# Layer-norm sums over partitions issued for four feature tiles together, one on each quarter of the TensorE array

## Chip, cores and metric

One core of one Trainium2 chip runs the whole program. The metric is the device time of one execution in microseconds (us): the median over several runs. All times below are in us unless marked ns.

## What is computed

The network has two post-norm layers over 256 latent and 256 context tokens with 1024 features. Each layer mixes tokens (a gated linear recurrence, an attention and a Mamba-2 scan, then one output projection) and then applies a SwiGLU feed-forward network (FFN). After each of the two sub-layers the residual stream goes through a layer norm over the 1024 features:

```python
def layer_norm(x, g, b):
    mu = jnp.mean(xf, axis=-1, keepdims=True)
    var = jnp.mean(jnp.square(xf - mu), axis=-1, keepdims=True)
    return ((xf - mu) * lax.rsqrt(var + LN_EPS) * g + b).astype(x.dtype)
...
# x <- LayerNorm(alpha * x + gate * sublayer(x * (1 + scale) + shift))
```

So there are four layer norms in the program. Only the latent tokens are needed behind the attention of the second layer.

## The kernel before, in words

Activations lie feature-major: a feature tile has 128 features on the partitions and the tokens along the free dimension, and 8 such tiles make the 1024 features. In layer 0 a tile has 512 columns (context and latent), in layer 1, behind the mixer, 256 (latent alone). Matrix products are made exact by splitting both operands into two float32r parts (`hh`/`hl`, `yh`/`yl`, `oh`/`ol` for activations, `wh`/`wl` for weights), with three products for each pair. Weight blocks of 128 x 1024 stream in by DMA from the SP queue (line 115) and are split by ACT (line 125, `wh`) and DVE (line 126, `wl`) some blocks ahead. All matmuls are issued by the helper in line 204, all transposes by that in line 208, so that rows are told apart by their tiles.

A layer norm reduces over partitions, which DVE can't. `ln_add` (line 1176) is called once for each feature tile, as soon as the tile of the residual sum has been made from PSUM by DVE (`resid`, line 1145, two scalar_tensor_tensor, one for each half of the tokens). The projection before it makes two tiles at a time, so tiles 0 and 1 come together, then 2 and 3, and so on. Nothing happens for the first three calls. At the fourth, `colmean` (line 880, with `quarters`, line 869) forms the mean of the first four tiles: four float32 matmuls with a 128 x 32 matrix of ones, each to another 32 partitions of one PSUM tile (`csum`), that is, on another quarter of the array's columns, then one matmul that adds the quarters. That mean (`pivot`) is taken off the four tiles and off what is added to the later ones. Then, tile by tile, ACT squares the tile (`sq`), and two float32 matmuls with the same 128 x 32 matrix of ones (`ones32`, printed `ones`) add over partitions: the tile into `lsum`, its square into `lsq`. Tile d goes to the quarter d % 4 of both PSUM tiles:

```python
            q = 32 * (d % 4)
            for ps, t in zip(ln["s"], (x, sq)):
                self.mm(ps[q:q + 32, 0:n], self.ones32, t, d < 4, d >= 4)
```

So a layer norm has 16 such sums, and the program 64. The first four tiles are summed in the fourth call, tiles 4 to 7 in one call each, with products of the projection between them. `raw_split` (line 405) then makes split operands of the tile (`raw`) for products that don't wait for the statistics.

`ln_stats` (line 1199) copies `lsum` (ACT) and `lsq` (DVE) to SBUF, adds the quarters with small matmuls into `lst`, and works out mean and inverse deviation with short DVE instructions (`s`). `ln_end` spreads them over partitions (`spread`). Meanwhile PE runs the products of `raw` (`g<-raw`), whose statistics are put in later. `post_norm` (line 1258) then normalizes tile by tile on DVE, applies gains on ACT and splits into `hh` and `hl` for the products of the next stage. After the first layer's second norm the first stage is the Mamba step sizes (`ssd_dt`, tiles `dx`, `dy`, `dz`), which end in two kinds of transposes on PE (`dtT`). After the last norm, `finish` (line 1369) makes the output token-major: products of the tiles with a diagonal of gains (`g<-dg`, `fin<-dg`), less the mean (`g<-gr,lsum`), scaled and stored.

The code is written as one stream with each engine's part in program order, but the order within each engine's queue is set by the tile framework's scheduler when the program is built: it moves instructions of an engine past each other by its own estimate of when they are ready. At run time each engine takes its queue strictly in that order, and an instruction whose inputs aren't there holds up all behind it.

Of the kernel before, what the change touches and what calls it, by code (L numbers as in the profile page):

```python
# [9 lines left out]
AF = mybir.ActivationFunctionType  # L10
# [5 lines left out]
ND = 8  # L16
# [4 lines left out]
T = SEQ + CTX  # L21
ALPHA = (2 * DEPTH) ** 0.25
FFN = 2816
# [10 lines left out]
# columns of the per-channel parameters of a layer  # L34
# [19 lines left out]
def stagger(a, b, n):  # L54
    """a, and from its step n on b beside it"""
    for _ in range(n):
        next(a, None)
        yield
    live = [a, b]
    while live:  # L60
        for g in list(live):
            if next(g, g) is g:
                live.remove(g)
            else:
                yield
# [6 lines left out]
class Weave:  # L72
    """Two strands of work: the steps of the side strand are spread over those of the main one and stay a
    little behind it, so that the main strand's next products never queue behind the end of a side chain."""
# [4 lines left out]
    def __call__(self, main, side, nm, ns, lead=0, lag=0):  # L79
        """nm and ns: the steps of each, lag: the part of the side strand, in steps of main, left for the next call"""  # L80
        side, n, j = chain(self.side, side), self.n + ns, 0
        for i, _ in enumerate(main):
            while j < n * (i + 1 - lead) / (nm - lead + lag):
                next(side, None)
                j += 1
        self.side, self.n = side, n - j
        if not lag:
            run(side)
            self.n = 0


class Weights:
    """Streams weight blocks [128, k, c] through SBUF: each block is loaded once
    and split into two float32r parts whose sum is the float32 value."""
# [49 lines left out]
class Net:  # L144
# [21 lines left out]
    def x(self, name="x"):  # L166
        """like a, for tiles that would otherwise queue behind the other strand's"""
        return self.wp.tile([P, 512], F32, tag="x", name=name, bufs=self.n_x)
# [45 lines left out]
    def rsqrt(self, x, n):  # L214
        """x <- x ** -1/2 on a few columns: a first guess from the exponent and three Newton steps"""
        y, t = self.s(n), self.s(n)
        self.ts(t.bitcast(I32), x.bitcast(I32), 1, ALU.arith_shift_right)
        self.ts(y.bitcast(I32), t.bitcast(I32), -1, ALU.mult, 0x5F3759DF, ALU.add)
        for i in range(3):
            self.stt(t, y, -0.5, y, ALU.mult, ALU.mult)  # L220
            self.tt(t, t, x, ALU.mult)
            self.stt(x if i == 2 else y, t, 1.5, y, ALU.add, ALU.mult)


# [37 lines left out]
    def lower_bounds(self):  # L262
        """the second layer's: the softmax over two layers as a sigmoid"""
        h = self.s(32)
        self.nc.gpsimd.dma_start(out=h, in_=self.io["lb"])
        self.tt(h[:, 0:16], h[:, 16:32], h[:, 0:16], ALU.subtract)
        self.act(self.lb, h[:, 0:16], AF.Sigmoid)
        self.act(self.lbm, h[:, 0:16], AF.Sigmoid, scale=-1.0)

# [1 line left out]
    def mod_spec(self, l, j, c):  # L271
        """512 columns from 512 j, rows [256 c, 256 c + 256)"""
# [27 lines left out]
    def tick(self):  # L300
        """a piece of the modulations that are needed later"""
# [10 lines left out]
    def load_x(self, d0, d1):  # L312
        """feature-major tokens, [context | latent]"""
# [8 lines left out]
    def modulate_first(self, d0, d1):  # L322
        """h = x (1 + sc) + sh"""
# [23 lines left out]
    def mm3(self, out, xh, xl, yh, yl, first, last):  # L347
        """out += (xh + xl)^T (yh + yl)"""
# [4 lines left out]
    def plan_w(self, key, w, cols, kt=ND):  # L353
        """a unit: 256 columns of a weight matrix, in blocks of four row tiles"""
# [5 lines left out]
    def unit_f(self, key, rng, x=None, kt=ND):  # L360
        """feature-major: two tiles of 128 columns by the tokens rng[m]"""
# [11 lines left out]
    def unit_raw(self, key, ln):  # L373
        """two tiles of 128 columns before the layer norm's statistics are there: products with the rows times
        the gains, and with the gains and biases as two more tokens"""
# [20 lines left out]
    def raw_end(self, ln, e, j):  # L396
        """the statistics put in: a tile but for the bias, and the bias"""
# [7 lines left out]
    def raw_split(self, ln):  # L405
        """the next rows times the gains as split operands, with the gains and biases behind them"""
# [17 lines left out]
    def unit_t(self, key, js):  # L424
        """token-major: pairs js of token tiles by 256 columns"""
# [23 lines left out]
    def hgrn_in(self, l, p, wc, st):  # L449
        """projections of a pair of heads and everything that reads them from PSUM"""  # L450
# [38 lines left out]
    def hgrn_head(self, l, st, m, wc, oh, ol):  # L489
        """One head: attention over all pairs of tokens by levels of halving. At level h a block of 2h tokens  # L490
        is halved; the forward direction reads keys of the first half from queries of the second, the
        backward direction the other way. K = [forward | backward] keys times the decay to the end
        (start) of their half, Q = [backward | forward] queries times the decay over their half."""
# [10 lines left out]
        def total(h):  # L504
            """products of the decays over blocks of h, [forward | backward] of T / h each"""
# [5 lines left out]
        def grow(h):  # L511
            """to halves of 2h"""
# [106 lines left out]
    def ssd_dt(self, l):  # L619
        """step sizes, their logarithms and the decays' running sums, (stream, direction, head) on partitions"""  # L620
# [30 lines left out]
        ln = r  # L651
# [49 lines left out]
    def conv(self, l, r, n, t0):  # L701
        """depthwise conv over time, feature-major"""
# [37 lines left out]
    def silus(self, tiles):  # L740
        """together, after the exponentials before them: one switch of the activation table"""
# [15 lines left out]
    def ssd_scan(self, l, g, st, dts, wc, ys):  # L757
        """both directions' scans of a group: within each stream by its decay matrix, from the context by its end states"""
# [85 lines left out]
    def ssd_out(self, l, g, ys, zs, wc, om):  # L844
        """gate and grouped RMS norm"""
# [23 lines left out]
    def quarters(self, tiles, n):  # L869
        """sum over partitions of every fourth tile, on 32 partitions each"""  # L870
# [9 lines left out]
    def colmean(self, tiles, n):  # L880
        """mean over partitions and tiles, on every partition"""
# [4 lines left out]
    def colrstd(self, tiles, n, scale, eps):  # L886
        """(scale * sum over partitions and tiles + eps) ** -1/2, on every partition"""
# [15 lines left out]
    def rms_tok(self, ps, scale):  # L903
        """(mean square + eps) ** -1/2 * scale of each 128 columns, [token, 4]"""
# [8 lines left out]
    def rotate(self, l, key, src, dst, lat):  # L913
        """gain, and on latent tokens rotary, of [token, (2 tiles, 2 heads, 128)]"""
# [13 lines left out]
    def attn_tables(self, l):  # L928
        """rotary tables with the gains in them"""
# [117 lines left out]
    def partial(self, key, o, dst, first, q0):  # L1047
        """dst += rows block of a projection; o is a function where it isn't there yet"""
# [23 lines left out]
    def gate_first(self, l, acc, q0):  # L1072
        """the gated Mamba branch, to DRAM"""
# [13 lines left out]
    def gates(self, l, br, q0, cs=range(4), f=AF.Sigmoid):  # L1087
        """the gates of a branch that isn't there yet, to DRAM"""
# [11 lines left out]
    def early(self, l, g=None):  # L1100
        """the gates (branch, columns) whose products stand beside the Mamba scan of group g, and all of them"""
# [4 lines left out]
    def gates_on(self, br, q0, cs):  # L1106
        """the sigmoids of gates that were stored before them"""
# [12 lines left out]
    def branch(self, l, br, key, o, q0, out=None):  # L1120
        """a gated branch added to those before it: to DRAM, or into split parts"""
# [23 lines left out]
    def resid(self, l, i, src, d, r, x, q0):  # L1145
        """r = gate * src + x"""
# [20 lines left out]
    PIVOT = 4  # L1167

    def ln_begin(self, q0, x, gains=None):
        """gains: of the layer norm and of what reads it"""  # L1170
        ln = {"q0": q0, "x": x, "r": [], "s": None, "raw": [], "ga": None}
# [4 lines left out]
    def ln_add(self, ln, r):  # L1176
        """The next tile of the rows to normalize. The mean of the first few is taken off all tiles as they
        come: what is left has a mean of the order of its deviation at most, and its sums give the variance."""
# [11 lines left out]
        for d in (range(np) if len(rs) == np else (len(rs) - 1,)):  # L1190
            x = rs[d][:, q0:T]
            sq = self.a(name="sq")[:, 0:n]
            self.act(sq, x, AF.Square)
            q = 32 * (d % 4)
            for ps, t in zip(ln["s"], (x, sq)):
                self.mm(ps[q:q + 32, 0:n], self.ones32, t, d < 4, d >= 4)
        self.raw_split(ln)

    def ln_stats(self, ln):
        """less the mean and the inverse deviation, [token, tile], and the sums they come from"""  # L1200
# [17 lines left out]
    def ln_end(self, ln):  # L1218
        """factor and summand of the normalization, token by token, on every partition"""
# [6 lines left out]
    def spread(self, x, nt):  # L1226
        """columns x [token, nt] to rows on every partition"""
# [11 lines left out]
    def gains(self, ln, l, ig, ib, nxt):  # L1239
        """the layer norm's own, times alpha, and those that lead to the input of what reads it"""  # L1240
# [18 lines left out]
    def post_norm(self, ln, raws):  # L1259
        """the units raws, and the split operand LN * (1 + sc) + sh of what reads it"""  # L1260
# [17 lines left out]
    def new_x(self, ln, q0):  # L1278
        """the residual stream alpha * LN"""
# [80 lines left out]
    def finish_tables(self, l):  # L1360
        """the last layer norm's gains on a diagonal, and its gains and biases as rows"""
# [7 lines left out]
    def finish(self, ln, out):  # L1369
        """the last layer norm, token-major: products with the diagonal of gains, less the mean times the gains"""  # L1370
# [165 lines left out]
def pack(inputs):  # L1536
    """the arrays of the launch: weights as they are, per-channel vectors and tokens with channels first"""
# [35 lines left out]
```

## Time and profile before

| | us |
|---|---|
| median of 3 runs | 2702.61 |
| fastest and slowest run | 2701.3, 2703.74 |
| the profiled execution, span from first to last instruction | 2706.7 |
| PE busy in it | 2619.4 |
| DVE busy | 1782.5 |
| ACT busy | 1232.1 |
| POOL busy | 192.4 |

The profile records one execution. No device time of it is given beside its span, which is 4.1 above the median of the runs. PE is the engine of matmuls, PEld its weight loads, which overlap. Matmuls are pipelined and their ends are modelled: distances between starts are the safe numbers. A float32 matmul of the kind above leaves two records, each with a weight load of its own. A name such as `lsum<-r,ones` says what is written and from what; xN is the number of records that a row merges.

### The profile page before, as it was taken

To read this page: it belongs to the slowest core of one execution; us is meant where nothing else is said; L and a number is where in the kernel's file an instruction comes from. 1 tells how busy PE (TensorE), PEld (TensorE's weight loads), DVE (VectorE), ACT (ScalarE), POOL (GpSimd) and SP (SyncE) were. 2 spreads that over 40 slices of the span, in tenths; PEclk is the share of its full clock that TensorE was granted. 3 is DMA by queue.
4 is the path that set the end of the run, shared out by engine and by line. 5 is a ranking of instruction groups with operands and counts; after the bars stand their busy time and mean duration, and the time that the engine had idled before them with its cause. 6 is when DMAs were issued, how large, how long until landed. Compare 5 with 4: busy or idle time off the path is not lost.

```text
span 2706.7 us, 46300 instructions
## 1 busy us (share of the span) xinstructions
PE 2619.4 (97%) x18660; PEld 2148.0 (79%) x18660; DVE 1782.5 (66%) x3708; ACT 1232.1 (46%) x2030; POOL 192.4 (7%) x320
## 2 busy tenths in 40 slices
PE   7999999999999999999999999899999999999999
PEld 5767767788888897777888877677878898878998
DVE  5887776756555675456433367887867778867555
ACT  3555554532333324535432236566554344465543
POOL 0111010000000001100000000111110011111000
PEclk9999999999999999999999999899999999999999
DMA  6566555543444445352333323555763353445553
GB/s 238 152 179 176 150 164 149 155 123 114 122 135 130 128 125 172 105 175 63 101 94 101 94 78 90 140 164 154 212 183 108 97 144 109 144 131 181 169 182 102
DMA packets 298951, 374.41 MB, mean 138 GB/s; under 512 B 16432, under 2 KB 251984, under 8 KB 298736
## 3 DMA queue, kind: packets, MB, share of 16 engines
q1 hardware_dynamic: 271568, 284.21, 34.9%
q0 software_dynamic: 25728, 84.61, 11.0%
q8 instruction: 147, 2.41, 0.4%
q10 hardware_dynamic: 1440, 2.62, 0.3%
q14 instruction: 68, 0.56, 0.1%
HBM read 355.27 MB, written 16.12 MB: 137 GB/s over the span
## 4 chain that ended last, share of the span: by engine, by line
PE 69%; DVE 6%; DMA 3%; ACT 3%; issue 1%; POOL 0%; DVEq 0%; ACTq 0%; SPq 0%
PE g L204 56%; PE y L204 1%; PE PV L204 1%; PE S L204 1%; DVE wl L126 1%; DMA wraw<-in_w_in 1%; DMA ce<-sd 1%; PE o L204 1%; PE small L204 1%; PE cross L204 1%; PE mod L204 1%; PE PT L208 1%; PE lsq L204 1%; DVE s L196 1%; ACT wh L125 1%
## 5 line engine op out<-in xcount | busy, mean ns | idle before, releaser
L126 DVE TENSOR_TENSOR wl<-wraw,wh 128x1024 fp32r<-128x1024 f32 (+1 forms) x450 | 544.5, 1212 | 430.2 <-ACT wh L125 419.3
L125 ACT ACTIVATE wh<-wraw 128x1024 fp32r<-128x1024 f32 (+1 forms) x450 | 470.9, 1048 | 712.0 <-PE g L204 513.1
L204 PE MATMUL g<-hh,wh 128*128 128x512 f32 (+2 forms) x2032 | 733.5, 363 | 5.4 <-ACT wh L125 2.1
L204 PE MATMUL g<-hh,wl 128*128 128x512 f32 (+2 forms) x2032 | 726.2, 358 | 4.4 <-DVE wl L126 4.4
L204 PE MATMUL g<-hl,wh 128*128 128x512 f32 (+2 forms) x2032 | 725.9, 358 | 0.0
L204 PEld LDWEIGHTS g<-hh,wh 128*128 128x128 f32 (+1 forms) x2032 | 387.9, 191 | 77.4 <-issue 16.0
L204 PEld LDWEIGHTS g<-hh,wl 128*128 128x128 f32 (+1 forms) x2032 | 388.4, 191 | 66.4 <-issue 9.1
L204 PEld LDWEIGHTS g<-hl,wh 128*128 128x128 f32 (+1 forms) x2032 | 388.6, 191 | 61.8 <-issue 12.1
L204 PE MATMUL g<-oh,wh 128*128 128x512 f32 (+1 forms) x864 | 301.3, 350 | 2.6 <-DVE gl L193 1.5
L204 PE MATMUL g<-ol,wh 128*128 128x512 f32 (+1 forms) x864 | 295.6, 343 | 0.2 <-DVE ol L196 0.2
L204 PE MATMUL g<-oh,wl 128*128 128x512 f32 (+1 forms) x864 | 293.1, 340 | 0.5 <-DVE wl L126 0.5
L204 PE MATMUL g<-wh,hh 128*128 128x256 f32 x768 | 221.4, 288 | 0.0
L204 PE MATMUL g<-wh,hl 128*128 128x256 f32 x768 | 220.0, 286 | 0.0
L204 PE MATMUL g<-wl,hh 128*128 128x256 f32 x768 | 218.7, 285 | 0.0
L204 PEld LDWEIGHTS g<-oh,wh 128*128 128x128 f32 x864 | 163.9, 190 | 30.0 <-issue 8.1
L204 PEld LDWEIGHTS g<-ol,wh 128*128 128x128 f32 x864 | 164.3, 190 | 23.4 <-issue 7.1
L204 PEld LDWEIGHTS g<-oh,wl 128*128 128x128 f32 x864 | 163.9, 190 | 21.0 <-issue 3.6
L204 PEld LDWEIGHTS g<-wh,hh 128*128 128x128 f32 x768 | 147.6, 192 | 3.1 <-issue 2.6
L204 PEld LDWEIGHTS g<-wh,hl 128*128 128x128 f32 x768 | 147.7, 192 | 2.2 <-issue 1.9
L204 PEld LDWEIGHTS g<-wl,hh 128*128 128x128 f32 x768 | 147.6, 192 | 0.5 <-issue 0.4
L196 DVE SCALAR_TENSOR_TENSOR u<-craw,vec,u 128x508 f32<-128x508 f32 (+3 forms) x192 | 131.0, 723 | 10.0 <-ACT u L190 8.9
L196 DVE SCALAR_TENSOR_TENSOR D<-ab,tk,neg 128x128 f32<-128x128 f32 x384 | 110.3, 347 | 21.5 <-DMA ab<-sd 21.5
(303 smaller groups left out, 3600.3 us busy)
## 6 DMA issues: line engine op xcount, KB each, us to landing
wraw<-in_w_in SPq DMA_DIRECT2D x216, 512.0 KB, 4.1
wraw<-in_w_mod SPq DMA_DIRECT2D x96, 512.0 KB, 4.1
wraw<-in_w_ffn_in SPq DMA_DIRECT2D x88, 512.0 KB, 3.6
ab<-sd POOLq DMA_DIRECT2D x64, 512.0 KB, 6.9
wraw<-in_w_ffn_out SPq DMA_DIRECT2D x40, 512.0 KB, 3.4
ce<-sd POOLq DMA_DIRECT2D x64, 256.0 KB, 7.6
wraw<-in_w_br_mb SPq DMA_DIRECT2D x32, 512.0 KB, 3.4
wraw<-in_w_in SPq DMA_DIRECT2D x34, 256.0 KB, 3.5
```

Of the source, the lines that this page charges most:

```text
L125: self.nc.scalar.activation(hi[:, 0:n], t[:, 0:n], AF.Copy)
L126: self.nc.vector.tensor_tensor(out=lo[:, 0:n], in0=t[:, 0:n], in1=hi[:, 0:n], op=ALU.subtract)
L196: return self.nc.vector.scalar_tensor_tensor(out=out, in0=a, scalar=s, in1=b, op0=op0, op1=op1)
L204: return self.nc.tensor.matmul(out, l, r, start=start, stop=stop)
L208: return self.nc.tensor.transpose(out, in_, self.ident[0:k, 0:k])
```

## The change

`ln_add` collects the squares, and issues no sums until a fourth tile is there (after the fourth call and after the eighth). Then it issues the four sums of the tiles, quarter after quarter, and the four sums of the squares after them. What is summed, into which PSUM tiles and on which quarters, is the same. Squares, pivot and `raw_split` are issued as before.

```diff
-        ln = {"q0": q0, "x": x, "r": [], "s": None, "raw": [], "ga": None}
+        ln = {"q0": q0, "x": x, "r": [], "s": None, "sq": [], "raw": [], "ga": None}
...
         for d in (range(np) if len(rs) == np else (len(rs) - 1,)):
-            x = rs[d][:, q0:T]
             sq = self.a(name="sq")[:, 0:n]
-            self.act(sq, x, AF.Square)
-            q = 32 * (d % 4)
-            for ps, t in zip(ln["s"], (x, sq)):
-                self.mm(ps[q:q + 32, 0:n], self.ones32, t, d < 4, d >= 4)
+            self.act(sq, rs[d][:, q0:T], AF.Square)
+            ln["sq"].append(sq)
+        if len(rs) % 4 == 0:
+            for ps, ts in zip(ln["s"], ([r[:, q0:T] for r in rs[-4:]], ln["sq"])):
+                for q, t in enumerate(ts):
+                    self.mm(ps[32 * q:32 * q + 32, 0:n], self.ones32, t, len(rs) == 4, len(rs) == ND)
+            ln["sq"] = []
         self.raw_split(ln)
```

The built order of the engines' queues shows what the scheduler made of it. The first place is PE's queue around tile 4 in the first norm of layer 0. Before, `r_11709` is tile 4 and `r_11723` tile 5, with their squares `sq_11712` and `sq_11726`; `g_11648` and `g_11737` are two tiles of the output projection:

```order
L204 MATMUL g_11648<-yh_11063,wl_11549 128x512
L204 MATMUL lsum_11601<-r_11709,ones32_87 32x512
L204 MATMUL lsq_11602<-sq_11712,ones32_87 32x512
L204 MATMUL lsum_11601<-r_11723,ones32_87 32x512
L204 MATMUL g_11737<-yh_11056,wh_11651 128x512
L204 MATMUL g_11737<-yl_11064,wh_11651 128x512
L204 MATMUL g_11737<-yh_11056,wl_11652 128x512
L204 MATMUL lsq_11602<-sq_11726,ones32_87 32x512
L204 MATMUL g_11737<-yh_11057,wh_11651 128x512
```

Now nothing stands there, and all eight sums stand behind the last product of the projection. `r_11709`, `r_11721`, `r_11795` and `r_11807` are tiles 4 to 7, on quarters 0 to 3:

```order
L204 MATMUL g_11734<-yh_11063,wl_11682 128x512
L204 MATMUL lsum_11601<-r_11709,ones32_87 32x512
L204 MATMUL lsum_11601<-r_11721,ones32_87 32x512
L204 MATMUL lsum_11601<-r_11795,ones32_87 32x512
L204 MATMUL lsq_11602<-sq_11712,ones32_87 32x512
L204 MATMUL lsum_11601<-r_11807,ones32_87 32x512
L204 MATMUL lsq_11602<-sq_11724,ones32_87 32x512
L204 MATMUL lsq_11602<-sq_11798,ones32_87 32x512
L204 MATMUL g_11895<-raw_11619,wh_11737 128x258
L204 MATMUL lsq_11602<-sq_11810,ones32_87 32x512
L204 MATMUL g_11895<-raw_11619,wh_11737 128x258
```

Seven of the eight sums became neighbours; the square of tile 7 stands alone, one product later. The second place is PE's queue at the end of the program, behind the last product of the FFN (`g<-oh,wl`), where tiles 6 and 7 of the last norm were summed one by one between the products of `finish`:

```order
L204 MATMUL g<-oh,wl 128x256
L204 MATMUL lsum<-facc,ones_87 32x256
L204 MATMUL g<-dg,facc 128x128 x2
L204 MATMUL lsq<-sq,ones_87 32x256
L204 MATMUL g<-dg,facc 128x128
L204 MATMUL lsum<-facc,ones_87 32x256
L204 MATMUL g<-dg,facc 128x128 x2
L204 MATMUL lsq<-sq,ones_87 32x256
L204 MATMUL g<-dg,facc 128x128
L204 MATMUL lst<-cmb,lsum 128x2 x2
```

```order
L204 MATMUL g<-oh,wl 128x256
L204 MATMUL lsum<-facc,ones_87 32x256 x3
L204 MATMUL lsq<-sq,ones_87 32x256
L204 MATMUL lsum<-facc,ones_87 32x256
L204 MATMUL lsq<-sq,ones_87 32x256 x2
L204 MATMUL g<-dg,facc 128x128
L204 MATMUL lsq<-sq,ones_87 32x256
L204 MATMUL g<-dg,facc 128x128
L204 MATMUL lst<-cmb,lsum 128x2 x2
```

Here too seven sums stand together and the last one alone. The queues of SP and POOL are unchanged; those of DVE and ACT are unchanged up to the statistics of each norm, and differ in order, not in content, for some hundred instructions behind the two norms of layer 0.

## Rows read from the trace of the kernel before

**Rows 1.** The page: busy time by engine, and the chain that ended last, by engine.

```profile
PE 2619.4 (97%) x18660; PEld 2148.0 (79%) x18660; DVE 1782.5 (66%) x3708; ACT 1232.1 (46%) x2030; POOL 192.4 (7%) x320
...
PE 69%; DVE 6%; DMA 3%; ACT 3%; issue 1%; POOL 0%; DVEq 0%; ACTq 0%; SPq 0%
```

**Rows 2.** Timeline (start, duration, engine, instruction): the pivot's sums, first norm.

```profile
1216.01 0.15 PEld L204 LDWEIGHTS csum<-r,ones 128*32 128x32 f32 x6 [0.35 <-issue]
1216.01 1.06 PE L204 MATMUL csum<-r,ones 128*32 128x512 f32 x6
...
1217.00 0.50 PE L204 MATMUL g<-yh,wh 128*128 128x512 f32 x1
...
1217.42 1.05 PE L204 MATMUL csum<-r,ones 128*32 128x512 f32 x2
...
1218.40 0.50 PE L204 MATMUL g<-yl,wh 128*128 128x512 f32 x1
```

**Rows 3.** Timeline of PE, first norm: the square of tile 5, alone.

```profile
1238.15 0.39 PE L204 MATMUL g<-yl,wh 128*128 128x512 f32 x1
1238.38 0.40 PE L204 MATMUL g<-yh,wl 128*128 128x512 f32 x1
1238.71 1.04 PE L204 MATMUL lsq<-sq,ones 128*32 128x512 f32 x2
1239.68 0.50 PE L204 MATMUL g<-yh,wh 128*128 128x512 f32 x1
1240.02 0.39 PE L204 MATMUL g<-yl,wh 128*128 128x512 f32 x1
```

**Rows 4.** Timeline of PE, first norm: the two sums of tile 6.

```profile
1249.79 0.39 PE L204 MATMUL g<-yh,wl 128*128 128x512 f32 x1
1250.11 1.05 PE L204 MATMUL lsum<-r,ones 128*32 128x512 f32 x2
1250.99 1.02 PE L204 MATMUL lsq<-sq,ones 128*32 128x512 f32 x2
1251.94 0.51 PE L204 MATMUL g<-raw,wh 128*128 128x258 f32 x2
```

**Rows 5.** Timeline of PE, third norm (256 columns): a square alone.

```profile
2476.04 0.28 PE L204 MATMUL g<-yh,wl 128*128 128x256 f32 x1
2476.25 0.62 PE L204 MATMUL lsq<-sq,ones 128*32 128x256 f32 x2
2476.80 0.39 PE L204 MATMUL g<-yh,wh 128*128 128x256 f32 x1
2477.02 0.28 PE L204 MATMUL g<-yl,wh 128*128 128x256 f32 x1
2477.14 0.28 PE L204 MATMUL g<-yh,wl 128*128 128x256 f32 x1
```

**Rows 6.** Timelines of DVE and ACT: what the sums wait for, first three norms.

```profile
1221.12 2.50 DVE L193 TENSOR_TENSOR r<-r,pivot 128x512 f32<-128x512 f32 x4 [2.92 <-ACT pivot L190]
...
1250.22 0.88 DVE L196 SCALAR_TENSOR_TENSOR r<-g,mod,xa 128x256 f32<-128x256 f32 x2 [0.15 <-PE g L204]
...
1630.53 1.65 DVE L196 SCALAR_TENSOR_TENSOR facc<-g,mod,facc 128x256 f32<-128x256 f32 x4
...
1631.98 0.61 ACT L190 ACTIVATE sq<-facc 128x512 f32<-128x512 f32 x1
...
2481.41 0.48 DVE L196 SCALAR_TENSOR_TENSOR r<-g,mod,xa 128x256 f32<-128x256 f32 x1 [0.24 <-PE g L204]
```

**Rows 7.** Timeline of PE behind the second norm; its waits behind the third.

```profile
1693.63 0.47 PE L208 MATMUL dtT<-ident,dy 128*128 128x128 f32 x1 [4.03 <-DVE dy L193]
...
1696.40 0.63 PE L204 MATMUL g<-hh,wh 128*128 128x512 f32 x1
1696.83 0.63 PE L204 MATMUL g<-hl,wh 128*128 128x512 f32 x1
...
PE g L204 <- ACT hh L190: 1.6, 2, 1.2
```

## The prediction

> **What bounds the kernel.** I read the page first: PE is busy 97% of the span and is 69% of the chain that ended last [rows 1]. So a microsecond less on PE counts almost fully, unless PE then waits for something that its own work hid so far. Then I read the timeline of PE around the sums, for the price of a sum, the timelines of DVE and ACT at the same places, for when the grouped sums can start, and last PE's waits behind the norms, for where the gain could be lost or grow.
>
> **The price of a sum.** Each 512-column sum leaves two records. Before it PE starts a product every 0.23 (1238.15 to 1238.38) [rows 3]. Around a sum that stands alone, the distance from the product before it to the second product behind it is 1240.02 - 1238.38 = 1.64, where two products take 0.46: a single costs 1.18 [rows 3]. Its own two passes are not the whole of it. Where a second sum follows on the same quarter, it is 1251.94 - 1250.11 = 1.83 from the first start to the next product [rows 4] against 1239.68 - 1238.71 = 0.97 for one [rows 3], so a further slot costs 0.86 and entering and leaving the narrow shape 1.18 - 0.86 = 0.32. A pair costs 2 x 0.86 + 0.32 = 2.04. With 256 columns a single costs 2477.02 - 2476.04 = 0.98 less two products of 0.12 (2477.02 to 2477.14), which is 0.74 [rows 5]; a further slot half of 0.86, 0.43; a pair 1.17.
>
> **What overlaps.** The pivot's sums have the form that the change gives to all sums: three neighbours on three quarters take 1217.00 - 1216.01 = 0.99 together, the fourth, alone, 1218.40 - 1217.42 = 0.98 [rows 2]. Three sums on different quarters cost one slot. The Trainium skill ("TensorE: Matmul & The Clock Gate", Part 3, The mechanism) says that weight loads overlap with matmuls in flight only when the row group differs; here all sums use all rows. By that rule the three could not have overlapped; the six weight loads of these three sums lie within the same 0.99 [rows 2], so I follow the trace and keep the rule as a rival. The same page (Part 3, Measured speedup) gives 2.38x for three column tiles of 512 columns. By that figure a slot of three would be 1.26 slots, about 1 us less gain over the four norms, an estimate from the page; the trace's three cost what one costs, and the sum goes by that.
>
> **The sum, norm by norm.** What the change moves are the eight sums of tiles 4 to 7. Now they are one block of two slots (three tile sums; then the squares of tiles 4 to 6 beside the sum of tile 7) and one single, because the square of tile 7 comes a little later in PE's order: 2.04 + 1.18 = 3.22 with 512 columns, 1.17 + 0.74 = 1.91 with 256, plus what the block waits for tile 7.
> First norm: before, a block of three sums (two slots), a pair and three singles, 2 x 2.04 + 3 x 1.18 = 7.62. In the new order tile 7 is wanted in the second slot, at about 1250.99, and DVE has it at 1250.22 + 0.88 = 1251.10: 0.1 of waiting [rows 4, 6]. Gain 7.62 - 3.32 = 4.3.
> Second norm: a block of two slots and five singles, 2.04 + 5.90 = 7.94. DVE makes tiles 6 and 7 from 1630.53 to 1632.18, so the block starts half way, at 1631.4, and the square of tile 6 is there only at 1631.98 + 0.61 = 1632.59 [rows 6], 0.3 behind the second slot; with a late start of 0.4 I take 0.7. Gain 7.94 - 3.92 = 4.0.
> Third norm: a pair and six singles, 1.17 + 4.44 = 5.61; tile 7 takes DVE 0.48 [rows 6], of which one slot of 0.43 hides most: 0.2. Gain 5.61 - 2.11 = 3.5.
> Last norm: a block of two slots and four singles, 1.17 + 2.96 = 4.13, and 2.11 now. Gain 2.0.
> Together 13.8.
>
> **Edits at nothing.** In the first four tiles the sums change places too, but the last one waits for DVE, which takes the pivot off four tiles in 2.50 until 1223.62 [rows 6], and the squares of tiles 2 and 3 stay singles. Zero, with one slot a norm either way as bounds: 2 x 0.86 + 2 x 0.43 = 2.6. The squares live longer, but every one is read before the next stage asks for buffers. Weight blocks, SP and POOL are untouched, and each weight block is split ahead of its products; were that cover gone, PE would wait for `wl` in front of a product of the next block, which I'd see at once.
>
> **What is late next.** Behind the second norm PE stands 4.03 for `dy`, the end of a chain of DVE and ACT work that starts with the norm's last sum; behind the third it waits 1.6 for `hh` [rows 7]. Both chains start earlier by more than PE does: in the second norm 23 products of `raw` stood ahead of the last sum, now 8, so the sum comes 15 x 0.12 = 1.8 earlier against the products, besides the singles it no longer queues behind. Of these waits of 5.6 I expect 2.2 to go (1.8 and 0.4). The bounds are 0, if the changed order of DVE and ACT behind those norms eats it, and 5.6. After the 4.03 wait products start 0.43 apart (1696.40 to 1696.83) instead of 0.23 [rows 3, 7], nearly half the pace, as at the lower of TensorE's two clocks. If the shorter wait spares it, each product there gains another 0.20; I count none, and 1.5 at the low end.
>
> **The time.** 13.8 + 2.2 = 16.0. The span of the profiled execution, 2706.7, becomes 2690.7; it stands 4.1 over the median of the runs, 2702.6, for which I say the same 16.0 less: 2686.6.
>
> **Rivals.**
> 1. No overlap: the sums of a group run one after the other. For it: nothing is saved by packing if weight loads of another quarter have to wait. Against: three sums in 0.99 [rows 2]. Then seven slots and a single cost 7 x 0.86 + 0.32 + 1.18 = 7.5 with 512 columns, 7 x 0.43 + 0.31 + 0.74 = 4.1 with 256; against 7.6, 7.9, 5.6 and 4.1 before that saves 0.1, 0.4, 1.5 and 0: 2 in all, 2700.6. The skill's rule on weight loads, above, would make it this. 4%.
> 2. Half is lost again: tile 7 or its square arrives behind more DVE or ACT work than today. Each norm could wait as long as one tile takes on both, 0.88 + 0.61 = 1.5 [rows 6], 6.0 in all instead of the 1.2 that I took, and the waits behind the norms stay as they are: 13.8 - 4.8 = 9.0 less, 2693.6. For it: PE takes its queue strictly in order, and the block stands in front of products that wait for nothing. Against: the order of DVE and ACT up to the statistics didn't change. 8%.
> 3. Slower: the block at the head of PE's queue waits for tile 7 so long that PE idles as it does for `dy` and comes back at the lower clock. At that place's price, 4.03 and some eight products at 0.20 more, 5.6 a norm, four norms lose 22.4 against 13.8: 2711. It decides from 3.5 of waiting a norm, five times what I find in the worst of the four. 2%.
> 4. The change doesn't do what it says, since the scheduler spreads the sums out again. The built order shows seven of eight as neighbours in all four norms, so this is left only for the first tiles, where I count nothing.
>
> **How the numbers follow.** The forecast has 86%. Its own range goes from 13.8 + 5.6 + 1.5 + 1 of the first tiles less (2680.7) to about 11 less, with the first tiles' bound against it and no wait shortened (2691.4). To hold 8 in 10 it is stretched to the second rival: 2680.5 to 2693.6. A measurement of this kernel can tell 0.2%, 5.4, from no change. Faster by more than that: the forecast and most of the second rival, 0.93; within it: the first rival and the rest, 0.05; slower: 0.02.
>
> **What the next profile would show.** If the steps are right, PE's timeline has four places where six or more `lsum` and `lsq` records stand together behind the last product of a projection, the block takes about 2 us with 512 columns and 1.2 with 256, and the stretch of tiles 4 and 5 shows products 0.23 or 0.12 apart without a break. The idle time in front of `dtT` is shorter than 4.03. A wrong overlap shows as starts of `lsum` on different quarters 0.43 apart or more instead of nearly together; a late tile 7 as idle time of PE inside the block, released by DVE or ACT; a chain lost by the new order as a longer wait for `dy` or `hh`. If the sum of these is right and the time isn't, the gain went into waits further on, and the list of PE's waits has a new line.

## The result and the profile after

The changed kernel takes 2682.28 (median of 4 runs, 2681.5 to 2684.12) against 2703.18 for the kernel before on the same chip (2701.3 to 2704.98). The ratio is 0.9927 with a 95% interval of [0.9914, 0.994]: 0.7% faster, 20.9 less, 4.3 under the forecast of 2686.6 and inside its range. The profiled execution took 2684.12, with a span of 2682.3.

Page of the kernel after: busy time by engine, and the chain that ended last, by engine.

```profile
PE 2599.6 (97%) x18660; PEld 2142.4 (80%) x18660; DVE 1782.8 (66%) x3708; ACT 1232.6 (46%) x2030; POOL 192.4 (7%) x320
...
PE 81%; DVE 8%; DMA 6%; issue 2%; ACT 2%; POOL 0%; SPq 0%; ACTq 0%; DVEq 0%; POOLq 0%
```

Against [rows 1] the number of instructions is the same on every engine, DVE and ACT are busy as long as before, and PE is busy 19.8 less. PE is 81% of the chain, so it still sets the end.

Timeline of PE, kernel after, first norm: the block of tiles 4 to 7.

```profile
1244.18 1.06 PE L204 MATMUL lsum<-r,ones 128*32 128x512 f32 x6
1245.06 0.59 PE L204 MATMUL lsq<-sq,ones 128*32 128x512 f32 x1
1245.22 0.62 PE L204 MATMUL lsum<-r,ones 128*32 128x512 f32 x1
1245.23 0.86 PE L204 MATMUL lsq<-sq,ones 128*32 128x512 f32 x3
1245.67 0.59 PE L204 MATMUL lsum<-r,ones 128*32 128x512 f32 x1
1245.68 0.60 PE L204 MATMUL lsq<-sq,ones 128*32 128x512 f32 x2
1246.21 0.39 PE L204 MATMUL g<-raw,wh 128*128 128x258 f32 x1
1246.53 1.04 PE L204 MATMUL lsq<-sq,ones 128*32 128x512 f32 x2
1247.50 0.39 PE L204 MATMUL g<-raw,wh 128*128 128x258 f32 x1
```

Seven sums, 14 records on four quarters, stand in 1246.21 - 1244.18 = 2.03 from first start to the next product. A pair on one quarter took 1.83 by the same measure [rows 4]. Three sums start before the first square (1244.18 to 1245.06, 0.88), and the sum of tile 7 and a square on another quarter start 0.01 apart. The square of tile 7 is alone and takes 0.97, as the single of [rows 3] did. The 0.2 over a pair is the wait for tile 7, 0.1 by the prediction. With 256 columns the block takes 1.21 in both norms of layer 1 (2460.34 to 2461.55 and 2668.30 to 2669.51, same timeline), where a pair takes 0.98 by this measure: 0.2 of waiting, as the prediction took.

In the second norm the same block is longer. Timeline of PE, kernel after:

```profile
1619.88 1.42 PE L204 MATMUL lsum<-facc,ones 128*32 128x512 f32 x6
1620.76 0.59 PE L204 MATMUL lsq<-sq,ones 128*32 128x512 f32 x1
...
1622.41 0.51 PE L204 MATMUL g<-raw,wh 128*128 128x258 f32 x2
```

It takes 2.53, 0.70 more than a pair. ACT squares tile 6 only at 1620.77, for 0.61 (timeline of ACT, next fence), so its sum waits to 1621.4. The prediction allowed 0.7 there [rows 6].

```profile
1620.77 0.61 ACT L190 ACTIVATE sq<-facc 128x512 f32<-128x512 f32 x1
```

Behind that norm PE still waits for `dy`. Timeline of PE, kernel after, to be held against [rows 7]:

```profile
1681.08 0.48 PE L208 MATMUL dtT<-ident,dy 128*128 128x128 f32 x1 [3.27 <-DVE dy L193]
1681.56 0.79 PE L204 MATMUL g<-hh,wh 128*128 128x512 f32 x1
1682.15 0.63 PE L204 MATMUL g<-hl,wh 128*128 128x512 f32 x1
1682.58 0.63 PE L204 MATMUL g<-hh,wh 128*128 128x512 f32 x1
```

The wait fell from 4.03 to 3.27 only, and products behind it are 0.43 apart as before.

### The profile page after: what moved, and what is told of

The parts are those of the page before. It is cut to its first block, busy times and chain, and to the rows that moved or that the text cites. A ratio compares the mean times of both kernels' runs of the same rounds, so it can differ in the third digit from the quotient of the medians.

```text
span 2682.3 us, 46304 instructions
## 1 busy us (share of the span) xinstructions
PE 2599.6 (97%) x18660; PEld 2142.4 (80%) x18660; DVE 1782.8 (66%) x3708; ACT 1232.6 (46%) x2030; POOL 192.4 (7%) x320
## 3 DMA queue, kind: packets, MB, share of 16 engines
q8 instruction: 147, 2.41, 0.4%
## 4 chain that ended last, share of the span: by engine, by line
PE 81%; DVE 8%; DMA 6%; issue 2%; ACT 2%; POOL 0%; SPq 0%; ACTq 0%; DVEq 0%; POOLq 0%
PE g L204 66%; DMA ce<-sd 2%; PE y L204 2%; DMA ab<-sd 2%; PE mod L204 2%; DVE wl L126 1%; PE PV L204 1%; PE S L204 1%; PE o L204 1%; DMA wraw<-in_w_in 1%; PE small L204 1%; PE cross L204 1%; PE csum L204 1%; DMA wraw<-in_w_mod 1%; PE PT L208 1%
```

## Where the time went: seven stretches that repeat

Two profiles of different kernels differ by what was changed and by what varies anyway. To part them I took the starts of the same PE records in every profile: the first pivot sum (`csum`) of each norm, the first product of `hh` behind it, the first `dtT`, and the end. Seven stretches between them, with their sum, and the two stretches that are left, ahead of the first norm and from `dtT` to the third norm (the Mamba scans and attention of the second layer):

| kernel (profile) | norm 1 to `hh` | `hh` to norm 2 | norm 2 to `hh` | `hh` to `dtT` | norm 3 to `hh` | `hh` to norm 4 | norm 4 to end | sum of seven | ahead of norm 1 | `dtT` to norm 3 |
|---|---|---|---|---|---|---|---|---|---|---|
| before | 64.56 | 322.44 | 58.88 | 31.73 | 36.09 | 178.46 | 30.68 | 722.85 | 1216.0 | 767.9 |
| before_again | 64.53 | 322.44 | 58.85 | 31.79 | 36.15 | 178.51 | 30.70 | 722.97 | 1218.1 | 760.4 |
| after | 59.77 | 321.35 | 54.96 | 31.09 | 32.57 | 178.34 | 28.20 | 706.28 | 1213.9 | 762.1 |
| after_again | 59.75 | 321.32 | 54.96 | 31.07 | 32.55 | 178.40 | 28.20 | 706.26 | 1214.2 | 760.6 |
| after_third | 59.75 | 321.31 | 54.93 | 31.07 | 32.56 | 178.41 | 28.22 | 706.25 | 1215.4 | 758.9 |
| layer0_only | 59.75 | 321.32 | 54.96 | 31.08 | 36.11 | 178.53 | 30.69 | 712.44 | 1214.2 | 765.7 |
| layer1_only | 64.56 | 322.45 | 58.84 | 31.79 | 32.55 | 178.39 | 28.21 | 716.80 | 1215.8 | 762.4 |
| one_quarter | 63.52 | 321.24 | 58.22 | 29.39 | 34.14 | 175.61 | 29.83 | 711.93 | 1217.4 | 766.4 |
| last_four_only | 59.76 | 321.32 | 54.94 | 31.08 | 32.57 | 178.43 | 28.20 | 706.31 | 1219.0 | 764.2 |
| last_four_again | 59.75 | 321.29 | 54.95 | 31.07 | 32.59 | 178.40 | 28.19 | 706.25 | 1216.8 | 764.0 |
| first_later | 56.64 | 321.36 | 51.84 | 31.11 | 30.07 | 178.26 | 26.10 | 695.38 | 1211.8 | 763.0 |
| all_at_end | 55.03 | 321.25 | 51.04 | 29.83 | 29.69 | 178.26 | 25.03 | 690.14 | 1218.2 | 763.0 |
| all_end_again | 55.00 | 321.25 | 51.06 | 29.82 | 29.69 | 178.19 | 25.03 | 690.03 | 1219.0 | 760.4 |

In each of the seven, profiles of the same code agree within 0.1; the last two columns range over 7 and 9. The change is worth 722.9 - 706.3 = 16.6: 4.8, 3.9, 3.5 and 2.5 in the norms (14.7), 1.1, 0.65 and 0.1 behind them (1.9). The medians moved by 20.9, so about 4 of it is left for the other two stretches. There PE, DVE, ACT and POOL run the same instructions (by name) in the same order in both kernels.

## Experiments

**after_again, layer0_only, layer1_only, one_quarter** ran together, against 2704.83 for the kernel before (14 runs, 2699.86 to 2710.86). after_again is the changed kernel as it is.

> The changed kernel once more, to see what varies from one execution to the next. My theory: the four norms gained 14.7 us on PE (4.8, 3.9, 3.5 and 2.5, as the two profiles show) and about 2 in the waits behind them; the rest of the 24.5 us between the two profiles (2.1 ahead of the first norm, 5.8 in the scans of layer 1, between the first dtT behind the second norm and the first pivot sum of the third) is variation of waits on DMA that has nothing to do with the sums. Then the time is again 2681 to 2685, but the stretch from that dtT to the third norm, 767.9 in the profile before and 762.1 after, comes out anywhere between 760 and 769. Rival: the 5.8 follow from the change (the stage meets other transfers at another time): then it is 762 within 1.

2683.9 (2681.26 to 2692.74), ratio 0.9928 [0.9905, 0.995]. The seven stretches repeat within 0.1. The stretch from `dtT` to norm 3 is 760.6, inside the theory's range and outside the rival's 762 within 1.

layer0_only groups the sums in the norms of layer 0 (512 columns) and takes the rest tile by tile; layer1_only has `not (q0 > 0)` for the condition.

```diff
-        if len(rs) % 4 == 0:
+        if not (q0 == 0):
+            for d, sq in zip(range(len(rs) - len(ln["sq"]), len(rs)), ln["sq"]):
+                q = 32 * (d % 4)
+                for ps, t in zip(ln["s"], (rs[d][:, q0:T], sq)):
+                    self.mm(ps[q:q + 32, 0:n], self.ones32, t, d < 4, d >= 4)
+            ln["sq"] = []
+        elif len(rs) % 4 == 0:
```

> Grouped sums in the two norms of layer 0 alone. My theory: 4.8 + 3.9 on PE and about 2 in the waits behind the norms, 10.7 less than before: 2691 to 2694, with a stretch from the first dtT to the third norm's pivot anywhere between 760 and 769. If the further gain in the scans follows from the earlier start: about 2687, with a stretch of 762.

2689.67 (2687.84 to 2694.08), ratio 0.9946 [0.9929, 0.9963]; sum of seven 712.44, 10.5 less than before. The time falls between the theory's 2691 to 2694 and the other's 2687; the stretch from `dtT` to norm 3, 765.7, is the theory's.

> Grouped sums in the two norms of layer 1 alone: up to the third norm every queue is as before. My theory: 3.5 + 2.5 less than before, 2696 to 2699. The stretch from the first dtT to the third norm's pivot has the same instructions in the same order as before: if it comes out well under 767.9, it varies by itself; if it is 768 within 1 here and 762 in the others, the gain there belongs to the change in layer 0.

2696.92 (2690.0 to 2705.09), ratio 0.9973 [0.9961, 0.9985]; sum 716.80, 6.1 less than before. So 10.5 + 6.1 = 16.6: the two layers add up, and each carries its own norms' gain. Up to the third norm layer1_only is the kernel before, yet its stretch from `dtT` to norm 3 is 762.4 where that of the first profile of before is 767.9: a stretch shorter by that much needs no change in the sums.

one_quarter keeps the eight sums of tiles 4 to 7 as neighbours, but puts all of them on quarter 0.

```diff
-                    self.mm(ps[32 * q:32 * q + 32, 0:n], self.ones32, t, len(rs) == 4, len(rs) == ND)
+                    p = 32 * q if first else 0
+                    self.mm(ps[p:p + 32, 0:n], self.ones32, t, first, q > 0 if first else q == 3)
```

> The eight sums of tiles 4 to 7 stay neighbours, but all go to the same quarter, so that none can overlap. If overlap on the quarters is what pays: eight slots, 8 x 0.86 + 0.32 = 7.2 us a norm with 512 columns and 3.75 with 256, against 3.4, 3.9, 2.1 and 2.1 in the changed kernel, so 10.4 us more: about 2693, and up to 3 more where the statistics come later. In the first norm the block from its first sum to the next product takes 7.0 instead of 2.0. If it is enough that the sums are neighbours (fewer switches between narrow and full products): no slower than the changed kernel, 2682 to 2685.

2691.4 (2689.5 to 2697.46), ratio 0.9952 [0.9934, 0.9969], near the 2693 expected without overlap and clear of 2682 to 2685. Timeline of PE of this kernel, first norm:

```profile
1251.12 3.60 PE L204 MATMUL lsq<-sq,ones 128*32 128x512 f32 x8
1254.65 1.05 PE L204 MATMUL lst<-cmb,lsum 128*128 128x2 f32 x8
```

Four squares take 1254.65 - 1251.12 = 3.53, 0.88 each, one behind the other. On four quarters seven sums took 2.03 in all. So the overlap comes from the quarters, not from standing together: the four norms (64.56, 58.88, 36.09 and 30.68 before) are 63.52 + 58.22 + 34.14 + 29.83 = 185.7 here against 175.5 in the change, 10.2 more, with 10.4 expected. The three stretches behind the norms give 4.5 of this back (526.2 together, 530.8 in the change), for two reasons that are not the sums themselves. Behind the second norm, 1.7: in PE's order 7 other products stand between those that make `dx`, where the change has 21, so `dx` starts 7.35 behind the first product of `hh` instead of 9.68. Behind the third norm, 2.7: PE waits no less there (0.2, 0.2, 1.0, 0.2 and 1.4, against 0.8, 0.5, 1.2 and 0.5 in the change), but it stays at 2.4 GHz, where the change spends part of the time at 1.2, and all of the 2.7 arises within the first 12: the 40th product behind the first of `hh` starts 11.50 after it in the change and 8.66 here. Granted clock of PE (window, length, PE busy, clock, DMA share, GB/s), the change first, then one_quarter, at the same place of the program:

```profile
2475.00:2485.00 10.00, 7.69 (x39) 0.83 0.60 176
```

```profile
2490.00:2500.00 10.00, 8.23 (x53) 1.00 0.54 168
```

This is one profile of one_quarter; that the clock would come out so again is not shown.

**last_four_only, first_later, all_at_end** ran together, against 2702.42 (9 runs, 2699.18 to 2707.74). last_four_only has the diff of layer0_only with the condition `not (len(rs) > 4)`.

> The first four tiles are summed tile by tile as before, tiles 4 to 7 together as in the change. Theory: the whole gain comes from tiles 4 to 7, since the first four tiles' sums wait for DVE's pivot work and ACT's squares either way. The time is the change's within 2 us (2681 to 2685), and each norm's last sum starts as soon behind its first pivot sum as in the change, within 0.5. Rival: the neighbours in the first four tiles carry a slot or two a norm as well; then up to 2.6 us of the gain is missing over the four norms and the time is 2685 to 2687, with 0.9 more in each norm of 512 columns between the pivot and the products behind it.

2688.63 (2684.18 to 2691.29), ratio 0.9946 [0.9933, 0.9959]. By the time alone the rival would stand, and more than it asked for is missing. But all seven stretches are the change's within 0.1, where the rival wanted 0.9 more in norms 1 and 2. I ran it again below.

first_later issues the eight sums of the first four tiles in the sixth call, two tiles later, as one block:

```diff
-        if len(rs) % 4 == 0:
-            for ps, ts in zip(ln["s"], ([r[:, q0:T] for r in rs[-4:]], ln["sq"])):
+        if len(rs) in (6, 8):
+            o = len(rs) // 8 * 4
+            for ps, ts in zip(ln["s"], ([r[:, q0:T] for r in rs[o:o + 4]], ln["sq"][o:o + 4])):
```

> The eight sums of the first four tiles are issued in the sixth call, when all their squares are long there, so that they can be one block of two slots a quarter; tiles 4 to 7 as in the change. Theory: with nothing to wait for inside it, that block costs 2.04 with 512 columns and 1.17 with 256, against some 5 and 3 for what stands there now in singles, pairs and waits; it takes some 3 us off each norm of layer 0 and 2 off each of layer 1, 8 to 10 in all, and the time is 2672 to 2676. Rival 1: what stands there now hides the waiting for the pivot and the squares, which PE pays anyway, because raw products or the next tiles aren't ready either; then the time is the change's within 2. Rival 2: a longer hold of the squares' buffers makes ACT or DVE late in tiles 4 to 7; then idle time of PE shows up inside the second block and the time is over the change's.

2673.11 (2671.93 to 2680.56), ratio 0.9896 [0.9882, 0.991]. The first block in the first norm, timeline of PE of this kernel:

```profile
1225.96 1.06 PE L204 MATMUL lsum<-r,ones 128*32 128x512 f32 x8
1226.84 1.04 PE L204 MATMUL lsq<-sq,ones 128*32 128x512 f32 x8
1227.81 0.50 PE L204 MATMUL g<-yh,wh 128*128 128x512 f32 x1
```

Eight sums take 1227.81 - 1225.96 = 1.85, where a pair took 1.83 [rows 4]. The four norms are 3.1, 3.1, 2.5 and 2.1 shorter than in the change, 10.8, a little over the 8 to 10 expected; neither rival shows.

all_at_end issues all sixteen sums in the eighth call:

```diff
-        if len(rs) % 4 == 0:
-            for ps, ts in zip(ln["s"], ([r[:, q0:T] for r in rs[-4:]], ln["sq"])):
+        if len(rs) == ND:
+            for ps, ts in zip(ln["s"], ([r[:, q0:T] for r in rs], ln["sq"])):
```

> All sixteen sums of a norm are issued in the eighth call, the four sums of tiles 0 to 3, of tiles 4 to 7, and then the squares' likewise: four slots a quarter. Theory: 4 x 0.86 + 0.32 = 3.8 with 512 columns and 4 x 0.43 + 0.31 = 2.0 with 256, against some 8.6 and 5.4 for both blocks of the change, 16 us less over the four norms; but the statistics come one or two slots later against the products, and behind the second and third norm, where PE waits for their chain, 0 to 4 are given back: 2666 to 2672. Rival: the longer block at the end delays the statistics by its whole length in all four norms, with nothing left to cover their chain; then the waits for dx, dy and hh behind the norms grow by what the block saves, and the time is the change's within 3, 2680 to 2686.

2673.3 (2668.92 to 2674.39), ratio 0.9887 [0.9872, 0.9903]. Timeline of PE of this kernel, first norm:

```profile
1243.23 2.08 PE L204 MATMUL lsum<-r,ones 128*32 128x512 f32 x16
1244.97 2.06 PE L204 MATMUL lsq<-sq,ones 128*32 128x512 f32 x16
1246.96 1.05 PE L204 MATMUL lst<-cmb,lsum 128*128 128x2 f32 x8
```

Sixteen sums take 1246.96 - 1243.23 = 3.73. The sum of seven is 690.1, 16.1 below the change: 14.7 in the norms, where 16 was worked out ahead, and 1.4 behind them, where nothing was given back. `hh` to `dtT` is 1.3 shorter, since PE's order has 11 other products between those that make `dx` instead of 21. The median stays above the expected 2666 to 2672 all the same: by the stretches it should lie 5 under first_later's, and it doesn't.

**before_again, after_third, last_four_again, all_end_again** ran together, against 2704.87 (13 runs, 2699.83 to 2707.32), to see what varies. None has an edit of its own.

> The kernel before once more, to see which of its stretches vary from one execution to the next. Theory: the seven stretches from each norm's first pivot sum to its first product of hh, and the ones between the norms of layer 0 and behind the third norm, repeat within 0.2 each: 64.6, 322.4, 58.9, 31.7, 36.1, 178.5 and 30.7, together 722.9; only the stretch ahead of the first norm (1211.8 to 1219.0 in the profiles so far) and that from the first dtT to the third norm (760.6 to 767.9) differ, and the median is 2700 to 2706. Rival: the seven stretches scatter by some us too, and then a difference of 16 us between kernels in them is worth no more than that of the medians.

2702.23 (2695.72 to 2707.74), ratio 0.999 [0.998, 1.0001]. The seven stretches come back at 722.97. Only the two others differ: from `dtT` to norm 3 it is 760.4, 7.5 shorter than in the first profile of the same kernel. PE's waits in the Mamba scans of the second layer show part of it, before first and before_again second (total, times, longest):

```profile
PE y L204 <- DVE M L193: 7.9, 5, 3.7
```

```profile
PE y L204 <- DVE M L193: 5.6, 2, 2.9
```

> The changed kernel a third time, beside last_four_again on the same chip. Theory: its seven stretches sum to 706.3 within 0.2, as in its first two profiles (706.28 and 706.26), and its median lies 16.6 below that of the kernel before, give or take the 4 us by which the other two stretches vary: 2682 to 2690. Rival: the change also shortens one of the two stretches that vary, by 4 us; then the median stays 20 or more below that of the kernel before, a third time.

2684.39 (2682.36 to 2691.44), ratio 0.9932 [0.9915, 0.9949], sum 706.25. The median is 20.5 under the kernel before, a third time; here the rival stands by its own test. The part beyond 16.6, about 4, came with each of the three runs of the changed kernel, and doesn't come from the norms. It is not much more than the 2.6 by which the kernel before differs from itself in before_again (2702.23 against 2704.87).

> The first four tiles tile by tile, tiles 4 to 7 together, once more. Its first run had a median of 2688.6, 6 above the change's, though its seven stretches (706.31 together) are those of the change. Theory: that was variation, and the median is now within 4 of after_third's, on either side. Rival: the first four tiles' order costs some 5 us somewhere outside the norms; then the median is again 4 to 7 above after_third's.

2688.67 (2684.79 to 2688.87), ratio 0.9936 [0.9921, 0.9951], sum 706.25. That is 4.3 above after_third, so this rival stands by its test too. By the stretches the first four tiles carry nothing; the difference lies in the two stretches that vary (together 1983.2 and 1980.8 in its two profiles, 1974.3 to 1976.0 in the three of the change). PE, DVE, ACT and POOL have the same order in both kernels there, so no queue shows where the rival's cost would lie.

> All sixteen sums of a norm in its eighth call, once more. In its first profile the seven stretches sum to 690.1, 16.1 below the change's. Theory: 690.1 again within 0.3, and a median 10 to 20 below after_third's. Rival: first_later (sum 695.4) is as good, since their medians were alike (2673.3 and 2673.1); then the median is within 2 of 2673 and the seven stretches don't tell the time.

2671.8 (2666.75 to 2679.33), ratio 0.9879 [0.9861, 0.9898], sum 690.03. The stretches repeat, and the median is 12.6 below after_third's, as the theory had it. It is also within 2 of first_later's 2673, as the rival had it, but the two ran beside different runs of the kernel before: 33.1 under theirs here, 29.3 for first_later and 29.1 for all_at_end. The 5.3 by which the stretches differ can neither be seen nor be excluded in 4 and 5 runs that range over 5 to 13. Both beat the change; which of the two is better by the time stays open.

## Why the prediction was right

**The price of a sum and the overlap: right.** A pair's cost for a block of two slots was the core of the sum [rows 2, 4]. The blocks took 2.03 and 2.53 with 512 columns, 0.2 and 0.7 over a pair, the waits for tile 7 and for the square of tile 6 that the prediction put at 0.1 and 0.7. The rule that weight loads overlap only when the row group differs (Trainium skill, "TensorE: Matmul & The Clock Gate", Part 3, The mechanism) would have made it one_quarter's price on any quarter. The trace disagrees: eight sums on four quarters in 1.85, each with all rows, two slots' worth. The 2.38x that the Trainium skill gives for three column tiles (same page, Part 3, Measured speedup vs the span model) is under what stands here, three sums in a slot of 0.88 (1244.18 to 1245.06) and four in the same 0.88 (1225.96 to 1226.84).

**The four norms: 13.8 predicted, 14.7 measured.** Second and third, 4.0 and 3.5, came out at 3.9 and 3.5. The first and the last were sized too small, 4.3 against 4.8 and 2.0 against 2.5, for one reason: I priced the block of three or four sums of tiles 4 and 5 in the kernel before as two full slots without a wait. Timelines of PE and DVE of the kernel before, first norm, and then last norm:

```profile
1235.40 1.04 PE L204 MATMUL lsum<-r,ones 128*32 128x512 f32 x2
1236.29 1.02 PE L204 MATMUL lsq<-sq,ones 128*32 128x512 f32 x2
1236.31 0.48 DVE L196 SCALAR_TENSOR_TENSOR r<-g,mod,xa 128x256 f32<-128x256 f32 x1
1236.84 1.04 PE L204 MATMUL lsum<-r,ones 128*32 128x512 f32 x2
1237.81 0.50 PE L204 MATMUL g<-yh,wh 128*128 128x512 f32 x1
...
2685.84 0.87 DVE L196 SCALAR_TENSOR_TENSOR facc<-g,mod,facc 128x256 f32<-128x256 f32 x2
2686.38 0.86 PE L204 MATMUL lsum<-facc,ones 128*32 128x256 f32 x3
2686.83 0.61 PE L204 MATMUL lsq<-sq,ones 128*32 128x256 f32 x2
2687.07 0.38 PE L204 MATMUL lsum<-facc,ones 128*32 128x256 f32 x1
2687.29 0.59 PE L204 MATMUL lsq<-sq,ones 128*32 128x256 f32 x2
2687.81 0.39 PE L204 MATMUL g<-oh,wh 128*128 128x256 f32 x1
```

The third sum of the first block, that of tile 5, starts at 1236.84 instead of beside the square at 1236.29, since DVE has the tile only at 1236.31 + 0.48 = 1236.79. So the block is 2.41 long where two slots are 1.83: 0.58 more. In the last norm DVE has tile 5 at 2686.71, its sum misses the first slot, and its square needs a third: the block is 1.43, against 0.98 for a pair (1.17 less the 0.19 or so that lie outside first start and next product): some 0.45 more. The two, less 0.1 more of waiting in the new block of the first norm, are the 0.5 by which each gain was too small.

**Rivals.** None of them took over: overlap is there (first), the blocks wait 0.2 and 0.7 in layer 0 and 0.2 in layer 1, where the second needed 1.5 a norm and the third 3.5, and the sums stay together (fourth).

**First four tiles at zero: right in the stretches.** last_four_only has them in the old order, and each norm is the change's within 0.05. Their block holds waits either way; first_later took those waits out and got 10.8.

**Behind the norms: 2.2 predicted, 1.9 measured, but elsewhere.** I gave 1.8 to the wait for `dy`, which shrank by 0.76, and 0.4 to those for `hh` behind the third norm, which stayed (1.6 before, 1.7 after; that stretch lost 0.1). Instead 1.1 went between the first norm and the second, where I had counted nothing: a stall around 1290, of which the timeline of PE of the kernel before shows a wait of 0.43 for `hh`, is absent after. So the near agreement of 1.9 with 2.2 is luck.

```profile
1291.58 0.73 PE L204 MATMUL g<-hh,wh 128*128 128x512 f32 x2 [0.43 <-ACT hh L190]
```

The step that failed here is that the sum's lead of 1.8 would reach `dy`. The lead is there when DVE begins to normalize, and it ends at `dx`. Timelines of DVE and PE behind the second norm's `spread`, before first and after second; `g<-hh,wl 128*64` is the last product that `dx` needs:

```profile
1647.34 2.47 DVE L193 TENSOR_TENSOR facc<-facc,spread 128x512 f32<-128x512 f32 x4
...
1671.16 0.39 PE L204 MATMUL g<-hh,wl 128*64 128x512 f32 x1
1671.59 0.97 DVE L200 TENSOR_SCALAR dx<-g,vec 64x256 f32<-64x256 f32 x2 [0.17 <-PE g L204]
...
1693.15 0.42 DVE L193 TENSOR_TENSOR dy<-dr,dx 128x256 f32<-128x256 f32 x1
```

```profile
1633.65 4.26 DVE L193 TENSOR_TENSOR facc<-facc,spread 128x512 f32<-128x512 f32 x7
...
1659.24 0.39 PE L204 MATMUL g<-hh,wl 128*64 128x512 f32 x1
1659.67 0.97 DVE L200 TENSOR_SCALAR dx<-g,vec 64x256 f32<-64x256 f32 x2 [0.50 <-PE g L204]
...
1680.61 0.42 DVE L193 TENSOR_TENSOR dy<-dr,dx 128x256 f32<-128x256 f32 x1
```

DVE's first normalizing instruction stands 1659.24 - 1633.65 = 25.59 ahead of that product, where it stood 1671.16 - 1647.34 = 23.82: 1.8 more, the lead as worked out. But DVE waits for the product in both kernels, and `dx` starts 0.43 behind it in both. From the second norm's pivot to its wait for `dy`, PE itself waits for nothing but 0.2 for `spread`, so this product comes when PE's queue reaches it, however early the statistics are. The prediction's chain from the norm's last sum to `dy` left out that it passes through PE's own queue. What the wait did lose was gained later: `dx` to `dy` is 1680.61 - 1659.67 = 20.94 instead of 1693.15 - 1671.59 = 21.56, 0.6 less. DVE's queue has another order there; that this is the cause is read from the queues, and no run undid it alone. The lower bound that the prediction gave, a changed order of DVE and ACT that eats the lead, is not what happened.

**The median: 20.9 where 16.0 was said.** The mechanisms give 16.6. The rest is not settled. That the two stretches vary by themselves is shown by before and before_again (767.9 and 760.4). The excess of 4 came with the changed kernel three times and not with last_four_only, whose engines run the same order there, which would speak for something fixed when a kernel is built. But it is small against the scatter: the kernel before differs from itself by 2.6 in before_again, and by the mean of all runs (40 of the kernel before, 12 of the change) the change gains 19.7, with 2.3 either way at 95%, so the excess is 3 rather than 4, and may be anything from 1 to 5. No run tells what it is. The ratio's interval, 16 to 23 of 2703, holds 16.6.

## What to carry to other kernels

Small sums over partitions with 32 columns of ones are cheap in groups: four neighbours on four quarters cost one slot (0.88 with 512 columns), and a lone one pays a slot and the 0.32 of a change of shape. Such a group should stand where its last operand is long ready, which is worth as much again: sixteen sums at the end of a norm took 3.73, and that beat the change by 16 in the stretches. A chain that starts earlier gains nothing where it next needs a product that stands at the same place of a busy queue. Before a gain of some us is credited to an edit, compare stretches between fixed records over several profiles; here that resolved 0.1 where medians resolved 4.

## What the runs showed that I had not expected

How long PE stays at the lower of its two clocks behind a wait is not told by the length of the wait. Granted clock of PE by stretch (window, length, PE busy, clock, DMA share, GB/s) behind the wait for `dy`, before first, then after, then after_third, the same kernel as after:

```profile
1693.60:1696.50 2.90, 2.87 (x7) 0.50 0.22 54
1696.50:1699.00 2.50, 2.50 (x8) 0.51 0.00 0
1699.00:1702.00 3.00, 2.87 (x14) 1.00 0.69 86
```

```profile
1681.00:1684.00 3.00, 2.92 (x7) 0.50 0.20 52
1684.00:1687.00 3.00, 3.00 (x9) 0.50 0.00 0
1687.00:1690.00 3.00, 3.00 (x9) 0.50 0.36 46
```

```profile
1682.40:1685.40 3.00, 2.76 (x7) 0.55 0.20 52
1685.40:1688.40 3.00, 3.00 (x13) 0.88 0.00 0
1688.40:1691.40 3.00, 2.37 (x14) 1.00 0.80 127
```

Behind a wait of 4.03 PE is at 1.2 GHz for 5.4 and then back at 2.4, and before_again repeats that. Behind the change's 3.27 it stays at the lower level for the whole 9 shown, and in after_again too; in after_third, behind a wait of 3.28 in the same kernel, it is back at 2.4 GHz before the 9 are over. At the lower level products start 0.43 apart instead of 0.23, so this may be one of the things that make the stretch from `dtT` to norm 3 vary; how much of it shows in the time isn't read here, since PE soon waits for other things.
